# One decoder step on one core: the order of the projections before the attention, four accumulator banks for them, and a tanh written in place

## The chip, the cores and the metric

The kernel runs on one core of a Trainium2 chip. The metric is the device time of one execution in microseconds. Five engines work side by side, each through its own instructions in order: TensorE (PE: matrix products and transposes), VectorE (DVE), ScalarE (ACT), GpSimd (POOL) and SyncE (SP), which issues the DMA transfers.

## The reference

One layer of a decoder is computed for a new sequence of 1024 tokens and for 8 single tokens with caches. After an RMS norm, one projection gives all streams; a recurrence (RG-LRU) and a dilated attention run in parallel, each is gated, and both are merged:

```python
proj = xn @ w_in
u, z_rnn, q, k, v, z_attn, g_rnn, g_attn = jnp.split(proj, split_points(), axis=-1)
uc, conv_new = causal_conv(u, conv_buf, conv_w, conv_b)
h, h_last = rg_lru(uc, h0, lru_w_a, lru_b_a, lru_w_x, lru_b_x, lru_lambda)
y_rnn = (h * jax.nn.silu(z_rnn)) @ w_rnn_out
...
y_attn = (y_attn * jax.nn.silu(z_attn)) @ w_attn_out
mixed = jax.nn.sigmoid(g_rnn) * y_rnn + jax.nn.sigmoid(g_attn) * y_attn
out = rms_norm(mixed @ w_out, norm_post)
```

Everything is float32. u, z_rnn and the two gates have 1024 columns each, z_attn 512, and q, k, v 1536 each.

## The kernel before

**Stripes.** The 1032 tokens lie along the free axis. A projection is worked off in *stripes* of 128 columns of `w_in`. A stripe is 8 contraction steps times three chunks of tokens (256, 384 and 392 wide; four chunks of about 256 for the first stripes), and each step is three matmuls (`mm3`, line 146), since both operands are split into a rounded part and a rest (`whi`, `wlo`; `xh`, `xl`): 72 matmuls a stripe, 24 a chunk, 12 a half chunk. ScalarE and VectorE make `whi` and `wlo` out of the loaded weights (`wraw`, lines 225 and 226) one or two stripes ahead.

**Accumulators.** A chunk is summed in one of the eight PSUM banks. `ps_tile` hands them out by tag: 2 banks `pj` for the projections, 3 `s` and 2 `pt` and 1 `o` for the recurrence and the attention. A chunk's bank is free again when the chunk has been read: by one ScalarE copy for u (line 540), by a ScalarE sigmoid for a gate (line 1109), by a ScalarE sigmoid and a VectorE product for z and z_attn (lines 549/550 and 686/687).

**The chains.** The recurrence is four *chains* of two 128-channel blocks (`chain`, `chain_front`). A chain convolves u, computes two gates from it (12 pairs of matmuls into `ps_s`, each read by two ScalarE sigmoids, line 601), multiplies on POOL (line 606), takes tanh, exp and square roots on ScalarE (lines 608, 623, 627), some products on VectorE and POOL, and a scan on VectorE (line 641). ScalarE loads another function table (ACT_TABLE_LOAD) when it changes between sigmoid, exp and square root.

**What sets the order.** The program is recorded in one pass; each engine then runs its part in the recorded order. The stripes are the main line. Beside it lie *lanes* (generators: a chain, an attention head pair, a merge, the decoder's sample rows), and every `yield n` in a lane says that its next step is due n planner nanoseconds later. The planner's clock `clk` advances with every recorded matmul, by a cost formula in `mm`; `tick`, called once per half chunk, records every lane step that is due.

**Slots.** All working tiles lie in 42 equal slots (`Arena`). When none is free, `Arena.get` calls `force`, which records the next lane step at once, due or not, until a slot comes free:

```python
    def get(self, shape, dtype, name):
        while not self.slots:
            self.pump()
```

**The stages.** In the opening, four stripes of u run while the four token groups are normalised and transposed. Then come z 0 to 3, u 4 and 5, z 4 and 5, u 6 and 7, z 6 and 7, the four z_attn stripes, 6 gate stripes, 36 stripes of v, k, q with the attention of the head pairs in the lanes, 10 gate stripes, and the three output projections. Gates are spilled to memory and loaded again later.

## Time and profile before

| | |
|---|---|
| median of 3 runs | 1291.03 us (1291.01 to 1292.82) |
| the profiled execution: its own time | 1294.25 us |
| the profiled execution: span, first to last instruction | 1292.5 us |
| mean granted TensorE clock | 0.987 |
| busy: PE, DVE, ACT, POOL | 1258.5, 604.6, 553.2, 221.9 us |
| DMA over the span | mean 97 GB/s |

PE is busy for 97% of the span, so nearly all of the time is matmul work, and the rest of the time is found by asking where PE stands still or runs at a lower clock. Busy shares of the other engines are averages over stages that differ much from each other.

### The profile page before, as it was taken

What the parts mean: (1) busy time and instruction counts of PE and PEld (TensorE: products, weight loads), DVE (VectorE), ACT (ScalarE), POOL (GpSimd) and SP (SyncE); (2) the same over time, 40 slices, a digit from 0 to 9 for tenths busy, and PEclk for the clock granted to TensorE, in tenths of its full rate; (3) what the DMA queues carried; (4) which work ended last, traced back from release to release, by engine and by line L of the source; (5) the groups of instructions that cost most, each with busy time, mean ns of one, the idle gap of its engine ahead of it and who ended that gap; (6) DMA issues with size and microseconds to landing.
All of it is one profiled execution on the core that took longest, in us unless ns stands there. A gap on an engine that the chain in (4) does not pass through costs nothing.

```text
span 1292.5 us, 21498 instructions
## 1 busy us (share of the span) xinstructions
PE 1258.5 (97%) x8726; PEld 1209.8 (94%) x8726; DVE 604.6 (47%) x1323; ACT 553.2 (43%) x1231; POOL 221.9 (17%) x232
## 2 busy tenths in 40 slices
PE   8999999799999999999999999999999999999997
PEld 8999998789999989999999999999999999998997
DVE  5552472761574274544256324643345245554226
ACT  6536636445539744334334344333652331222222
POOL 5000221311220131150026001420026000002001
PEclk9999999899999999999999999999999999998999
DMA  7210130232330133632074016512365474223115
GB/s 234 67 33 17 33 99 17 71 125 69 100 112 5 49 96 108 165 84 66 17 212 120 25 42 164 135 50 66 97 189 154 137 260 150 66 66 99 33 67 197
DMA packets 149449, 125.98 MB, mean 97 GB/s; under 512 B 8873, under 2 KB 135305, under 8 KB 149342
## 3 DMA queue, kind: packets, MB, share of 16 engines
q1 hardware_dynamic: 149350, 124.61, 32.0%
q8 instruction: 69, 1.13, 0.4%
q14 instruction: 30, 0.25, 0.1%
HBM read 98.44 MB, written 26.21 MB: 96 GB/s over the span
## 4 chain that ended last, share of the span: by engine, by line
PE 87%; ACT 5%; DVE 5%; issue 1%; DMA 1%; POOL 0%; SPq 0%; DVEq 0%; ACTq 0%
PE ps_pj L146 75%; PE ps_s L146 5%; PE ps_o L146 3%; PE ps_s L150 3%; PE ps_pt L150 2%; ACT gate L601 1%; DVE wlo L226 1%; DVE tanh L641 1%; ACT whi L225 1%; DMA wraw<-in_w_in 1%; DVE ck L1057 1%; ACT gate L623 1%; ACT sq L627 0%; ACT P L823 0%; ACT L627 0%
## 5 line engine op out<-in xcount | busy, mean ns | idle before, releaser
L146 PE MATMUL ps_pj<-xh,whi 128*128 128x256 f32 (+3 forms) x1760 | 574.7, 327 | 12.1 <-DVE za L687 11.0
L146 PE MATMUL ps_pj<-xl,whi 128*128 128x256 f32 (+3 forms) x1760 | 560.4, 318 | 0.0
L146 PE MATMUL ps_pj<-xh,wlo 128*128 128x256 f32 (+3 forms) x1760 | 560.1, 318 | 0.0
L146 PEld LDWEIGHTS ps_pj<-xh,whi 128*128 128x128 f32 x1760 | 334.0, 190 | 21.0 <-DVE za L687 12.4
L146 PEld LDWEIGHTS ps_pj<-xl,whi 128*128 128x128 f32 x1760 | 334.0, 190 | 0.2
L146 PEld LDWEIGHTS ps_pj<-xh,wlo 128*128 128x128 f32 x1760 | 333.6, 190 | 0.0
L226 DVE TENSOR_TENSOR wlo<-wraw,whi 128x512 fp32r<-128x512 f32 x176 | 149.6, 852 | 320.0 <-ACT whi L225 314.0
L225 ACT ACTIVATE whi<-wraw 128x512 fp32r<-128x512 f32 x176 | 109.6, 625 | 3.9 <-DMA wraw<-in_w_in 1.9
L823 ACT ACTIVATE P<-P,stat 128x128 f32<-128x128 f32 (+1 forms) x192 | 84.3, 440 | 53.0 <-DVE stat L819 52.9
L146 PE MATMUL ps_pj<-wlo,mh 128*128 128x256 f32 (+1 forms) x288 | 80.6, 286 | 0.1
L146 PE MATMUL ps_pj<-whi,mh 128*128 128x256 f32 x256 | 73.3, 286 | 2.7 <-ACT whi L225 2.7
L146 PE MATMUL ps_pj<-whi,ml 128*128 128x256 f32 x256 | 73.2, 286 | 0.0
L716 ACT ACTIVATE qt<-ps_pj,qsc 128x384 f32<-128x384 f32 (+1 forms) x36 | 27.6, 766 | 81.5 <-PE ps_pj L146 79.6
L146 PE MATMUL ps_pj<-hzh,wlo 128*128 128x256 f32 (+2 forms) x192 | 61.4, 320 | 0.0
L146 PE MATMUL ps_pj<-hzl,whi 128*128 128x256 f32 (+2 forms) x192 | 61.4, 320 | 0.0
L146 PE MATMUL ps_pj<-hzh,whi 128*128 128x256 f32 (+2 forms) x192 | 61.3, 319 | 0.0
L1109 ACT ACTIVATE sg<-ps_pj 128x256 f32<-128x256 f32 (+2 forms) x48 | 22.0, 458 | 91.7 <-PE ps_pj L146 90.4
L819 DVE CUSTOM_DVE_ANT_0 P<-ps_s,base 128x128 f32<-128x128 f32 (+1 forms) x192 | 56.0, 348 | 8.5 <-PE ps_s L146 8.0
L840 ACT ACTIVATE PT<-ps_pt 128x256 f32<-128x256 f32 (+1 forms) x48 | 21.0, 437 | 91.0 <-PE ps_pt L150 90.9
L601 ACT ACTIVATE gate<-ps_s,par 64x256 f32<-64x256 f32 (+2 forms) x96 | 52.1, 543 | 16.0 <-PE ps_s L146 14.4
L838 DVE COPY PT<-ps_pt 128x512 f32<-128x512 f32 (+1 forms) x48 | 28.7, 597 | 54.1 <-PE ps_pt L150 54.1
L146 PEld LDWEIGHTS ps_pj<-wlo,mh 128*128 128x128 f32 (+1 forms) x288 | 52.3, 181 | 0.5 <-DVE wlo L226 0.4
(247 smaller groups left out, 1690.1 us busy)
## 6 DMA issues: line engine op xcount, KB each, us to landing
wraw<-in_w_in SPq DMA_DIRECT2D x72, 512.0 KB
ck<-in_cache_kv_w SPq DMA_DIRECT2D x24, 512.0 KB
sgd<-sg SPq DMA_DIRECT2D x16, 516.0 KB
sgl<-sgd SPq DMA_DIRECT2D x16, 516.0 KB
xin<-in_x_prompt SPq DMA_DIRECT2D x16, 512.0 KB
qb<-sd SPq DMA_DIRECT2D x12, 512.0 KB
fb<-fd SPq DMA_DIRECT2D x24, 256.0 KB
hzd<-uc SPq DMA_DIRECT2D x8, 516.0 KB
```

Of the source, the lines that this page charges most:

```text
L146: nc.tensor.matmul(out, lhsT, rhs, start=start, stop=stop)
L150: nc.tensor.transpose(out, in_, idn)
L225: nc.scalar.activation(hi[:, a:b], raw[:, a:b], AF.Copy)
L226: nc.vector.tensor_tensor(lo[:, a:b], raw[:, a:b], f32(hi[:, a:b]), op=OP.subtract)
L601: nc.scalar.activation(G[gate][rows, cs], p[at:at + 64, :n], AF.Sigmoid, bias=par[rows, b, 5 + gate:6 + gate])
L623: nc.scalar.activation(R[b], R[b], AF.Exp, scale=spk[:, 1, b:b + 1])
L716: nc.scalar.activation(dst, src, AF.Copy, scale=C["qsc"][:, g, hp:hp + 1])
L819: nc.vector.tensor_tensor_reduce(out=pt[:, h, :128 * n], in0=ps[h][:, off:off + 128 * n], in1=base, scale=-SLOPES[g][2 * hp + h] * DIL[g], ...
L823: nc.scalar.activation(pt[:, h, :128 * n], pt[:, h, :128 * n], AF.Exp, scale=-1.0, bias=st[:, g, 0, h, b:b + 1], accum_out=st[:, g, 1, h, ...
L838: nc.vector.tensor_copy(t, src)
L840: nc.scalar.activation(t, src, AF.Copy)
L1109: nc.scalar.activation(z[:, c0:c0 + n], p[:, :n], AF.Sigmoid)
```

## The change

**Order.** The opening runs u 0, u 1 and two gate stripes. After it, the list `EARLY_BLOCKS` alternates pairs: z, u, gates, z, u, gates and so on, with the z_attn stripes among the last z and gate stripes. A chain is spawned after each second u stripe as before. Eight gate stripes (instead of six) come before the attention, eight (instead of ten) after it.

**Banks.** Outside the attention (`wide[0]` true) the projections' chunks take the banks in turn from two `pj` and the two `pt` banks; during the attention they have the two `pj` banks as before.

**tanh in place.** tanh is written into the tile `gi` of the input gate, which the POOL product reads just ahead of it; before, it went into a fresh slot and `gi` was freed.

**Planner.** `mm` now charges n/2.25 + 4 instead of n/2.4 planner nanoseconds for a matmul of n columns, and the gate steps of a chain are due 1000 instead of 1300 after one another.

```diff
--- before.py
+++ after.py
@@ -24,13 +24,18 @@
 WIN = (128, 512, 2048)
 COL_U, COL_Z, COL_Q, COL_K, COL_V = 0, 1024, 2048, 3584, 5120
 COL_ZA, COL_GR, COL_GA = 6656, 7168, 8192
-UZ = ((COL_U, (0, 1, 2, 3)), (COL_Z, (0, 1, 2, 3)), (COL_U, (4, 5)), (COL_Z, (4, 5)), (COL_U, (6, 7)), (COL_Z, (6, 7)))
 EPS = 1e-6
 BIG = 1e30
 NSLOT = 42
 WARM = 40
-EARLY_GATES = 6
 GATES = [(kind, b) for kind in range(2) for b in range(8)]
+LATE_GATES = 8
+
+FIRST = [("u", 0), ("u", 1), ("g", 0), ("g", 1)]
+EARLY_BLOCKS = [("z", 0), ("z", 1), ("u", 2), ("u", 3), ("g", 2), ("g", 3),
+                ("z", 2), ("z", 3), ("u", 4), ("u", 5), ("g", 4), ("g", 5),
+                ("z", 4), ("z", 5), ("u", 6), ("u", 7), ("g", 6), ("a", 0),
+                ("z", 6), ("z", 7), ("a", 1), ("a", 2), ("a", 3), ("g", 7)]
 STEP = 3400
 SPARE = 5
 KY, VY = 3000, 4000
@@ -78,7 +83,13 @@
     ar = Arena(arena_pool, NSLOT)
     new = ar.get
 
+
+    wide, turns = [True], [0]
+
     def ps_tile(tag):
+        if tag == "pj" and wide[0]:
+            turns[0] += 1
+            tag = ("pj", "pj", "pt", "pt")[turns[0] % 4]
         bufs = {"pj": 2, "s": 3, "pt": 2, "o": 1}[tag]
         return psum.tile([128, 512], F32, tag=tag, bufs=bufs, name="ps_" + tag)
 
@@ -140,7 +151,7 @@
         for q in out.shape[1:]:
             n *= q
         if rhs.dtype == F32R:
-            clk[0] += n / 2.4 if n >= 256 else max(4 * n / 2.4, 107)
+            clk[0] += n / 2.25 + 4 if n >= 256 else max(4 * n / 2.4, 107)
         else:
             clk[0] += max(4 * n / 2.4, 214) * (0.75 if out.shape[0] == 64 else 1.0)
         nc.tensor.matmul(out, lhsT, rhs, start=start, stop=stop)
@@ -171,19 +182,19 @@
     w_ao = I["w_attn_out"][0].rearrange("(k p) c -> p k c", p=128)
     w_oo = I["w_out"][0].rearrange("(k p) c -> p k c", p=128)
     WL = []
-    for base, bl in UZ:
-        for b in bl:
-            WL.append(w_in[:, :, base + 128 * b:base + 128 * b + 128])
-    for hp in range(4):
-        WL.append(w_in[:, :, COL_ZA + 128 * hp:COL_ZA + 128 * hp + 128])
-    for kind, b in GATES[:EARLY_GATES]:
-        WL.append(w_in[:, :, (COL_GA, COL_GR)[kind] + 128 * b:][:, :, :128])
+    for what, i in FIRST + EARLY_BLOCKS:
+        if what == "g":
+            kind, b = GATES[i]
+            c = (COL_GA, COL_GR)[kind] + 128 * b
+        else:
+            c = {"u": COL_U, "z": COL_Z, "a": COL_ZA}[what] + 128 * i
+        WL.append(w_in[:, :, c:c + 128])
     for hp in range(4):
         for g in range(3):
             for base in (COL_V, COL_K, COL_Q):
                 c = base + g * 512 + hp * 128
                 WL.append(w_in[:, :, c:c + 128])
-    for kind, b in GATES[EARLY_GATES:]:
+    for kind, b in GATES[-LATE_GATES:]:
         WL.append(w_in[:, :, (COL_GA, COL_GR)[kind] + 128 * b:][:, :, :128])
     for s in range(4):
         WL.append(w_ao[:, :, 256 * s:256 * s + 256])
@@ -600,13 +611,12 @@
                     at = 64 * (gate ^ s)
                     nc.scalar.activation(G[gate][rows, cs], p[at:at + 64, :n], AF.Sigmoid,
                                          bias=par[rows, b, 5 + gate:6 + gate])
-                yield 1300
+                yield 1000
         ar.free(*xs)
         R[b], gi = G
         nc.gpsimd.tensor_tensor(x, x, gi, op=OP.mult)
-        t = T[b] = new([128, NT], F32, "tanh")
-        nc.scalar.activation(t, R[b], AF.Tanh, scale=spk[:, 0, b:b + 1])
-        ar.free(gi)
+        T[b] = gi
+        nc.scalar.activation(gi, R[b], AF.Tanh, scale=spk[:, 0, b:b + 1])
 
     def chain(j):
         bl = (2 * j, 2 * j + 1)
@@ -1102,12 +1112,12 @@
 
     sgd = dram.tile([2, KB, 128, NT], F32, name="sgd")
 
-    def proj_g(kind, b):
+    def proj_g(kind, b, chunks=CHUNKS):
         z = new([128, NT], F32, "sg")
 
         def evac(c0, n, p):
             nc.scalar.activation(z[:, c0:c0 + n], p[:, :n], AF.Sigmoid)
-        yield from project(evac)
+        yield from project(evac, chunks)
 
         def spill():
             nc.sync.dma_start(sgd[kind, b], z)
@@ -1137,7 +1147,7 @@
     def turned(gi, k0=0):
         ahead[:] = [lambda k: k >= k0 and next(norm[gi], None)]
 
-    started = [proj_u(b, EARLY) for b in range(4)]
+    started = [proj_u(0, EARLY), proj_u(1, EARLY), proj_g(*GATES[0], EARLY), proj_g(*GATES[1], EARLY)]
 
     def half(i, n=1):
         for _ in range(n):
@@ -1189,20 +1199,12 @@
     clear_low_w()
     C = late_consts()
     spawn("lru", chain(0))
-    for b in range(4):
-        advance(proj_z(b))
-    spawn("lru", chain(1))
-    for j in (2, 3):
-        for b in (2 * j, 2 * j + 1):
-            advance(proj_u(b))
-        for b in (2 * j, 2 * j + 1):
-            advance(proj_z(b))
-        spawn("lru", chain(j))
+    for what, i in EARLY_BLOCKS:
+        advance({"u": proj_u, "z": proj_z, "a": proj_za}[what](i) if what != "g" else proj_g(*GATES[i]))
+        if what == "u" and i % 2:
+            spawn("lru", chain(i // 2))
     spawn("lru", state_out())
-    for hp in range(4):
-        advance(proj_za(hp))
-    for kind, b in GATES[:EARLY_GATES]:
-        advance(proj_g(kind, b))
+    wide[0] = False
     for hp in range(4):
         for g in range(3):
             for kind in (2, 1, 0):
@@ -1218,11 +1220,12 @@
         nc.sync.dma_start(t, sgd[kind, b])
         sgt[kind, b] = t
 
-    for i, (kind, b) in enumerate(GATES[EARLY_GATES:]):
-        if i == len(GATES) - EARLY_GATES - 2:
+    for i, (kind, b) in enumerate(GATES[-LATE_GATES:]):
+        if i == LATE_GATES - 2:
             until(lambda: len(merged) == 4 and len(sampled) == 4)
             spawn("split", split_ya())
-        if i == len(GATES) - EARLY_GATES - 3:
+            wide[0] = True
+        if i == LATE_GATES - 3:
             load_sg(0, 0)
             load_sg(0, 1)
         advance(proj_g(kind, b))
```

**Order on TensorE, second chain.** `uc2` is the convolved u split in two, `lh` and `low_w` the recurrence's weights, `whi`, `wlo`, `xh` and `xl` the projection's operands; the number at the end of a name counts tiles. Before, among the last pairs of gate matmuls of the second chain:

```order
L146 MATMUL ps_pj_2301<-xh7_24_123,wlo_124_2125 128x392
L146 MATMUL ps_s_2333<-uc2_120_2090,lh_1976 128x392
L146 MATMUL ps_s_2333<-uc2_120_2090,low_w0_135 128x392
L146 MATMUL ps_s_2341<-uc2_125_2174,lh_2035 128x392
L146 MATMUL ps_s_2341<-uc2_125_2174,low_w1_136 128x392
L146 MATMUL ps_s_2346<-uc2_121_2091,lh_1976 128x256
L146 MATMUL ps_s_2346<-uc2_121_2091,low_w0_135 128x256
L146 MATMUL ps_s_2351<-uc2_126_2175,lh_2035 128x256
L146 MATMUL ps_s_2351<-uc2_126_2175,low_w1_136 128x256
L146 MATMUL ps_s_2356<-uc2_121_2091,lh_1976 128x384
L146 MATMUL ps_s_2356<-uc2_121_2091,low_w0_135 128x384
L146 MATMUL ps_s_2361<-uc2_126_2175,lh_2035 128x384
```

Now, the chain's first pair:

```order
L157 MATMUL ps_pt_2158<-xh3_20_119,whi_117_2028 128x384
L157 MATMUL ps_pt_2158<-xl3_28_127,whi_117_2028 128x384
L157 MATMUL ps_pt_2158<-xh3_20_119,wlo_118_2029 128x384
L157 MATMUL ps_s_2175<-uc2_114_2006,lh_1906 128x256
L157 MATMUL ps_s_2175<-uc2_114_2006,low_w0_135 128x256
L157 MATMUL ps_pt_2158<-xh4_21_120,whi_117_2028 128x384
L157 MATMUL ps_pt_2158<-xl4_29_128,whi_117_2028 128x384
L157 MATMUL ps_pt_2158<-xh4_21_120,wlo_118_2029 128x384
L157 MATMUL ps_pt_2158<-xh5_22_121,whi_117_2028 128x384
```

Before, eight pairs in a row stand at this place without a projection matmul between them (`Arena.get` found no slot free there, in the first z_attn stripe). Now each pair is followed by the 12 projection matmuls of a half chunk, through the whole of the second chain.

**Order on ScalarE, after the gates of a chain.** `zs` and `za` are the z and z_attn chunks read from the accumulator; `ps_pj` or `ps_pt` names the kind of bank. Before, second chain:

```order
L601 ACTIVATE gate_133_2276<-ps_s_2371,par_114 64x392
L608 ACTIVATE tanh_136_2377<-gate_130_2253,spk_132 128x1032
L608 ACTIVATE tanh_137_2380<-gate_132_2275,spk_132 128x1032
L225 ACTIVATE whi_138_2382<-wraw_135_2339 128x512
L686 ACTIVATE za_134_2338<-ps_pj_2384 128x256
L623 ACT_TABLE_LOAD
L623 ACTIVATE gate_130_2253<-gate_130_2253,spk_132 128x1032
L623 ACTIVATE gate_132_2275<-gate_132_2275,spk_132 128x1032
L225 ACTIVATE whi_138_2382<-wraw_135_2339 128x512
L686 ACT_TABLE_LOAD
L686 ACTIVATE za_134_2338<-ps_pj_2415 128x384
L627 ACT_TABLE_LOAD
```

Now, the same chain:

```order
L612 ACTIVATE gate_129_2194<-ps_s_2390,par_114 64x392
L236 ACTIVATE whi_134_2353<-wraw_125_2128 128x512
L619 ACTIVATE gate_127_2174<-gate_126_2173,spk_132 128x1032
L619 ACTIVATE gate_129_2194<-gate_128_2193,spk_132 128x1032
L560 ACTIVATE zs_133_2352<-ps_pj_2395 128x384
L633 ACT_TABLE_LOAD
L633 ACTIVATE gate_126_2173<-gate_126_2173,spk_132 128x1032
L633 ACTIVATE gate_128_2193<-gate_128_2193,spk_132 128x1032
L560 ACT_TABLE_LOAD
L560 ACTIVATE zs_133_2352<-ps_pj_2428 128x392
L236 ACTIVATE whi_138_2460<-wraw_137_2458 128x512
L637 ACT_TABLE_LOAD
```

The functions and the reads of chunks come in the same pattern, with the tanh's output now named as a gate tile, and the chunks now come out of both kinds of bank.

**Order on ScalarE, opening.** `ext` is a chunk of u, `sg` a chunk of a gate, `xin` normalised rows, `xh0` to `xh2` the transposed ones that PE works with. Before:

```order
L243 ACTIVATE whi_47_334<-wraw_10_94 128x512 x2
L370 ACTIVATE xin_7_88<-xin_7_88,rstd_326 128x512 x2
L540 ACTIVATE ext_40_244<-ps_pj_313 128x256
L540 ACTIVATE ext_41_246<-ps_pj_359 128x256
L379 ACTIVATE xh0_17_116<-ps_s_388,gain_115 128x256
L379 ACTIVATE xh1_18_117<-ps_s_396,gain_115 128x256
```

Now:

```order
L254 ACTIVATE whi_45_330<-wraw_10_94 128x512 x2
L381 ACTIVATE xin_7_88<-xin_7_88,rstd_322 128x512 x2
L551 ACTIVATE ext_40_244<-ps_pt_309 128x256
L1119 ACT_TABLE_LOAD
L1119 ACTIVATE sg_47_353<-ps_pj_356 128x256
L390 ACTIVATE xh0_17_116<-ps_s_386,gain_115 128x256
L390 ACTIVATE xh1_18_117<-ps_s_394,gain_115 128x256
```

The read of the third stripe's chunk is a sigmoid now, with a table load ahead of it, and both stand ahead of the `xh` tiles. In the opening there are five such loads now after the first two of the program, and one before (line 504).

## Rows read from the trace of the kernel before

**Rows 1.** The page, part 1: busy time and share of the span.
```profile
PE 1258.5 (97%) x8726; PEld 1209.8 (94%) x8726; DVE 604.6 (47%) x1323; ACT 553.2 (43%) x1231; POOL 221.9 (17%) x232
```

**Rows 2.** What TensorE waited for: in total, times, longest.
```profile
PE ps_pj L146 <- DVE za L687: 11.0, 5, 4.9
PE ps_s L146 <- ACT gate L601: 2.7, 5, 0.7
PE ps_pj L146 <- ACT whi L225: 2.7, 1, 2.7
PE ps_pt L150 <- ACT P L823: 2.3, 2, 2.2
...
PE ps_pj L146 <- ACT ext L540: 0.6, 1, 0.6
```

**Rows 3.** Windows (us): length; busy (instructions) of PE, PEld, DVE, ACT, POOL; clock; DMA.
```profile
150.00:175.00 25.00, 25.00 (x159) 25.00 (x158) 19.95 (x24) 6.36 (x14) 11.05 (x6) 1.00 0.27 81
200.00:225.00 25.00, 22.32 (x131) 20.95 (x130) 3.50 (x6) 17.94 (x33) 3.38 (x2) 0.93 0.07 22
225.00:250.00 25.00, 18.16 (x102) 17.64 (x101) 15.93 (x14) 13.44 (x17) 8.52 (x4) 0.88 0.12 43
250.00:275.00 25.00, 21.05 (x123) 20.53 (x122) 20.18 (x26) 7.74 (x13) 8.74 (x12) 0.92 0.52 169
450.00:475.00 25.00, 22.57 (x158) 19.66 (x158) 19.36 (x45) 12.79 (x36) 6.70 (x4) 0.93 0.18 52
```

**Rows 4.** Timeline of ScalarE, second chain: start, us, instruction, [idle before <- releaser].
```profile
213.62 9.13 ACT L601 ACTIVATE gate<-ps_s,par 64x392 f32<-64x392 f32 x16
...
224.89 0.62 ACT L225 ACTIVATE whi<-wraw 128x512 fp32r<-128x512 f32 x1
...
225.79 1.28 ACT L623 ACT_TABLE_LOAD   x1
...
227.08 2.21 ACT L623 ACTIVATE gate<-gate,spk 128x1032 f32<-128x1032 f32 x2
```

**Rows 5.** Timelines of ScalarE and VectorE: one z_attn chunk behind a scan.
```profile
241.92 0.49 ACT L686 ACTIVATE za<-ps_pj 128x384 f32<-128x384 f32 x1 [3.85 <-PE ps_pj L146]
...
246.68 4.13 DVE L641 TENSOR_TENSOR_SCAN tanh<-gate,sq 128x1024 f32<-128x1024 f32 x1
...
251.59 0.55 DVE L687 TENSOR_TENSOR za<-ps_pj,za 128x384 f32<-128x384 f32 x1
```

**Rows 6.** Timelines of POOL and ScalarE: product and tanh, first chain.
```profile
134.22 2.42 POOL L606 TENSOR_TENSOR uc<-uc,gate 128x1032 f32<-128x1032 f32 x1 [0.31 <-ACT gate L601]
...
135.85 2.19 ACT L608 ACTIVATE tanh<-gate,spk 128x1032 f32<-128x1032 f32 x2
```

**Rows 7.** Timelines of ScalarE and TensorE, opening.
```profile
25.55 1.63 ACT L379 ACTIVATE xh<-ps_s,gain 128x256 fp32r<-128x256 f32 x3 [0.29 <-PE ps_s L150]
...
24.67 0.38 PE L146 MATMUL ps_pj<-xh,whi 128*128 128x256 f32 x1 [0.56 <-ACT ext L540]
```

**Rows 8.** Timelines of TensorE and ScalarE: one pair of attention blocks.
```profile
545.92 1.13 PE L146 MATMUL ps_s<-kt,qt 64*128 64x256 f32 x8
...
549.11 0.49 ACT L823 ACTIVATE P<-P,stat 128x256 f32<-128x256 f32 x1
...
551.77 1.04 PE L150 MATMUL ps_pt<-ident,P 128*128 128x128 f32 x8
```

**Rows 9.** Timeline of ScalarE, fourth chain within the attention.
```profile
448.77 2.02 ACT L627 ACTIVATE sq<-tanh 128x1032 f32<-128x1032 f32 x2
```

**Rows 10.** Timelines of POOL and VectorE: the decoder's value products.
```profile
826.86 5.74 POOL L1054 TENSOR_TENSOR ck<-ck,pT 128x1024 f32<-128x1024 f32 x3 [17.93 <-DVE yn L1047]
...
842.90 3.40 DVE L1057 TENSOR_TENSOR ck<-ck,ck 128x1024 f32<-128x1024 f32 x1
```

**Rows 11.** Chain of waits, in order of time: half chunks of 12 matmuls.
```profile
391.33 1.42 PE ps_pj L146 x12
...
392.99 2.11 PE ps_pj L146 x12
```

## The prediction

> **What bounds the kernel.** I read four views in turn. The page's first part: TensorE (PE) is busy for 97% of the span, the other engines for 47% at most [rows 1]. So a change that leaves the matmuls alone can only win what PE loses in waits and at a lower clock. PE's waits name the losses: 11.0 us in five waits for VectorE's product of a z_attn chunk, 2.7 us for the gates' sigmoids, 2.7 us for a `whi`, 2.3 us for the attention's exponentials, 0.6 us for a copy of u [rows 2]. The windows say where: between 200 and 275 us PE's busy time falls to 22.32, 18.16 and 21.05 of 25 us and the granted clock to 0.93, 0.88 and 0.92; before that, at 150 to 175 us, PE is busy throughout at clock 1.00 although VectorE is busy for 19.95 us [rows 3]. There is a second, smaller hole at 450 to 475 us. The timelines say why. Sixteen gate sigmoids stand in one block of 9.13 us on ScalarE [rows 4], because the order recorded the chain's last pairs of gate matmuls back to back. The chain's products and scans then follow as densely on VectorE: the sigmoid of a z_attn chunk ends at 242.4 us, but its product starts only at 251.59, behind a scan of 4.13 us that began at 246.68 [rows 5]. With two banks for the projections, PE cannot start the next chunk but one before that product is done.
>
> **The change, part by part.** The sum is made against the profiled execution's 1294.25 us; the median of the runs shown, 1291.03, lies 3.2 us lower, and I take the difference over to it.
>
> *The hole at 200 to 275 us.* At full pace a window holds 159 matmuls, 0.157 us each; these three hold 131, 102 and 123, so 477 - 356 = 121 are missing: 19.0 us [rows 3]. Of it 13.5 us is PE's idle time, the rest the clock. The new order has one pair of gate matmuls per half chunk through the whole second chain, so the block of sixteen sigmoids is gone, and with it the dense run of products behind it. The slots that it lacked come from the tanh in place (one a block, two a chain), and from gate stripes, whose tile leaves soon, between z stripes, whose tile stays until its chain ends. Bounds: nothing, if the same work blocks elsewhere; 19.0 if all comes back. I take 19.0 off, and put back what is left in the next item.
>
> *What is left of it.* ScalarE and VectorE have the same work for the chains. The longest stretch of ScalarE without a chunk's read is now `whi`, load, two square roots and load: 0.62 + 1.28 + 2.02 + 1.28 = 5.2 us [rows 4, 9]. Two banks let PE run ahead by one chunk, two half chunks of 1.42 to 2.11 us [rows 11]; four banks by three chunks, over 8.5 us. So PE does not wait for reads; it may wait for a `wlo` behind two scans of 4.13 us. I take 1.0 us; bounds 0 and 5.
>
> *The opening.* Two gate stripes there change their reads from copies to sigmoids, between groups whose norm needs a square root: four more table loads of 1.28 us [rows 4]. ScalarE is the pace there: it waits 0.29 us between `xh` tiles, and PE lives on them [rows 7]. The first load stands directly ahead of the `xh` of the second group and I count it whole; the others fall where ScalarE waits anyway. PE's wait of 0.56 us for a bank [rows 7] goes, with four of them. With half a microsecond for the other loads: +1.3 us; bounds -0.6 and 4 x 1.28 = 5.1. The Trainium skill ("ScalarE: Activation LUTs", What ACT_TABLE_LOAD costs) speaks against this edit: it says to group functions by table set, and puts a switch at about 2.66 us, load and drain. By that figure the four loads would come to 10.6 us, and the sum to 3.6 us saved. The trace does not agree on the second half: the load at 225.79 ends at 227.07 and the exponential starts at 227.08 [rows 4].
>
> *tanh in place.* ScalarE must now wait until POOL has read `gi`. In the first chain the second product runs from 134.22 to 136.64, so the first is done before that; the two tanh, 2.19 us together, start at 135.85 and so at about 136.9 [rows 6]: each after its product. Cost 0; bound, where the tanh come right behind the last gate: 0.31 + 2.42 less the first tanh's 1.1 and a `whi`'s 0.6, 1.0 us a chain. The cover is the four banks; in the fourth chain, with two, it is counted below.
>
> *The fourth chain and the first attention heads.* Before, PE loses 2.43 us of busy time and 7% of the clock in 25 us, 1.75 us, here: 4.2 us [rows 3]. The chain still runs into the attention. Now its tanh, exponentials and square roots stand between the exponentials of the first head pair's own blocks. Following ScalarE from the first scores in the new order: two gate sigmoids 1.1 (9.13 / 16 each), load 1.3, four exponentials 2.0 [rows 8], load 1.3, sigmoids 1.1, `whi` 0.6, two tanh 2.2 with an estimated wait of 1.0 for POOL (the bound above), a copy as long as an exponential 0.5, load 1.3, four exponentials 2.0 [rows 4, 6]: the second pair of blocks is ready after 14.4 us, and PE wants it after two turns of 4.7 us [rows 8], at 9.4. That is an estimated 5.0 us of waits less half a microsecond that the scores take, and the same 1.75 us of clock: about 6.3, so +2.1 us; with a little for the blocks behind the square roots I take +2.3. Bounds: -4.2 (fewer loads in all, and the hole closes) and +8.
>
> *The attention's pace.* The planner charged 256 / 2.4 = 107 ns for a matmul that takes 1.42 us / 12 = 118 [rows 11]; now it charges 118. So every lane step comes about a tenth sooner. A pair of blocks has 4.7 us between its scores' end (547.05) and its turn (551.77), and is ready at 549.6: 2.2 us of slack [rows 8], of which half a microsecond goes. Cost 0, bounds 0 and 4. In one head pair the order runs out of slots and takes three of the decoder's sample steps early; VectorE's sum of 3.40 us then waits for POOL's products, 5.74 us for three [rows 10]. It holds a chunk's copy and one pair's scores: +1.5 us, bounds 0 and 4.
>
> *After the attention.* Two gate stripes fewer (72 x 0.157 = 11.3 us each) cover the last merge; no wait of PE for it is among the rows of its waits, the largest of which are in [rows 2]. If that cover is gone, up to 3 us. Cost 0. The four banks there save nothing, since PE has no wait for a chunk's read left.
>
> **Sum:** -19.0 + 1.0 + 1.3 + 2.3 + 1.5 = -12.9 us: 1281.4 for a profiled execution, **1278** for the median of the runs.
>
> **The rivals.**
> - *More comes back* (0.15): the fourth chain's hole closes too, since the program has 6 table loads fewer around it. 1291.0 - 19.0 + 1.0 + 1.3 + 1.5 - 4.2 = 1272. For it: the loads, 1.28 us each [rows 4]. Against: ScalarE has the chain's and the attention's functions at once, with two banks.
> - *The jam moves* (0.12): ScalarE's and VectorE's work is the same, and half of the loss turns up at another chain: 9.5 less is saved, 1287.6. For it: VectorE at 20 of 25 us [rows 3]. Against: the first chain has such a window with no loss, and only two banks.
> - *The order is not relieved* (0.03): slots run out again later in the early stripes, the block returns, and the opening's and the attention's costs remain: about 1294. The order speaks against it.
> - *Slower, by the attention's pace* (0.04): if blocks become ready later than 2.2 us more than now, PE waits in each of the 48 turns. From 12.9 / 48 = 0.27 us a turn on, the gain is eaten; at 0.35 us it is 1295. For it: the lanes come sooner while a block's work stays. Against: slack of four times what is taken.
> - *Loads cost double* (0.03): ScalarE stands for as long again behind each of the opening's four loads, 8 x 1.28 = 10.2 us instead of 1.3: 1287. The two rows at 225.79 and 227.08 [rows 4] speak against it. This is the time by the Trainium skill's page named above.
>
> **How the numbers follow.** My forecast has 0.63, around 1278, from 1273 to 1284. The range 1269 to 1288 takes in the bounds of the unknown costs as far as they are likely together, and most of the first two rivals; the rest leave out some 0.17. A measurement of this kernel can tell about 0.2%, 2.6 us, from no change. Below 1288.4 lie the forecast, the first rival, two thirds of the second, and part of the last: 0.88. Within 0.2%: a third of the second, parts of the third and of the last: 0.07. Slower: the fourth and the rest: 0.05.
>
> **What would show it.** Right: the windows between 75 and 330 us all hold PE at 24.5 us or more at clock 1.00, the wait for the z_attn product is gone from PE's waits, no block of sixteen sigmoids is left; the opening's first four stripes end one to two microseconds later; PE's waits for exponentials near the first heads grow to some 5 us. Wrong: a window below 23 us in the early stripes (the jam moved), or many short waits of PE for exponentials through the attention (its pace).

## The result, and the profile after

The changed kernel takes **1279.71 us** (median of 4 runs, 1275.84 to 1280.51), the kernel before 1291.11 in the same comparison: a ratio of 0.9903, 95% interval 0.988 to 0.9925. It is faster by about 11 us. The profiled execution took 1279.06 us with a span of 1277.3. Against the span of before, 1292.5 us, that is 15.2 us less; the profiled execution of before lay 3.2 us above its median, which is why the spans differ by more than the medians.

The page, part 1, and what TensorE (PE) waited for, after; they answer to [rows 1] and [rows 2]:

```profile
PE 1251.2 (98%) x8726; PEld 1205.4 (94%) x8726; DVE 613.2 (48%) x1323; ACT 549.9 (43%) x1230; POOL 219.0 (17%) x232
```

```profile
PE ps_s L157 <- DVE ck L1067: 4.4, 1, 4.4
PE ps_s L161 <- DVE xl L391: 2.8, 2, 1.7
...
PE ps_s L161 <- DVE vn L769: 1.6, 1, 1.6
...
PE ps_pt L161 <- ACT P L833: 0.4, 1, 0.4
```

The 11.0 us for the z_attn product are gone, and so are the gates' 2.7 but for 0.8 and the exponentials' 2.3 but for 0.4. At the top stands a wait that is new: 4.4 us for `ck`, VectorE's sum of the decoder's value products (line 1067). Windows of after (columns as in [rows 3]):

```profile
200.00:225.00 25.00, 25.00 (x160) 25.00 (x159) 3.74 (x6) 17.59 (x31) 5.25 (x2) 1.00 0.31 97
225.00:250.00 25.00, 25.00 (x162) 25.00 (x161) 15.65 (x16) 14.41 (x21) 5.19 (x3) 1.00 0.10 30
250.00:275.00 25.00, 25.00 (x165) 25.00 (x164) 22.42 (x24) 10.07 (x18) 8.84 (x11) 1.00 0.41 127
...
450.00:475.00 25.00, 25.00 (x196) 22.51 (x195) 11.21 (x36) 10.38 (x33) 0.00 (x0) 1.00 0.33 91
...
975.00:1000.00 25.00, 20.62 (x107) 20.27 (x106) 14.48 (x11) 2.79 (x6) 10.86 (x4) 0.80 0.32 105
```

Both holes of [rows 3] are closed: the three windows from 200 us and the one at 450 us are full, at a granted clock of 1.00. A new hole is at 975 us, with a clock of 0.80. The same window of before had lost much less:

```profile
975.00:1000.00 25.00, 24.58 (x153) 24.19 (x152) 13.98 (x10) 3.92 (x8) 16.18 (x6) 0.93 0.41 129
```

**Where the time came from** is read from landmarks, instructions that both programs have. After has two gate stripes more ahead of the attention and two fewer behind it. One stripe takes 11.31 us, read from the same chunk of two gate stripes that follow each other, after:

```profile
967.31 0.49 ACT L1119 ACTIVATE sg<-ps_pj 128x384 f32<-128x384 f32 x1 [3.31 <-PE ps_pj L157]
...
978.62 0.49 ACT L1119 ACTIVATE sg<-ps_pj 128x384 f32<-128x384 f32 x1 [3.24 <-PE ps_pj L157]
```

So 22.6 us are allowed for the two. The landmarks are the last group's first `xh` (end of the opening), the first read of a query stripe, the read of the single tokens' queries in the 3rd, 10th, 11th and 12th query stripes, and the first product with `w_attn_out`. ScalarE's timeline and the tile `yah`, before:

```profile
49.04 0.48 ACT L379 ACTIVATE xh<-ps_s,gain 128x264 fp32r<-128x264 f32 x1
...
379.98 0.47 ACT L716 ACTIVATE qt<-ps_pj,qsc 128x256 f32<-128x256 f32 x1 [1.62 <-PE ps_pj L146]
...
491.68 0.22 ACT L718 ACTIVATE smp<-ps_pj 128x8 f32<-128x8 f32 x1
...
817.56 0.17 ACT L718 ACTIVATE smp<-ps_pj 128x8 f32<-128x8 f32 x1
...
868.35 0.22 ACT L718 ACTIVATE smp<-ps_pj 128x8 f32<-128x8 f32 x1
...
914.01 0.21 ACT L718 ACTIVATE smp<-ps_pj 128x8 f32<-128x8 f32 x1
...
L146 PE MATMUL ps_pj<-yah,whi x96: 274/337/345, 1042.5 to 1087.4; 128*128 128x256 f32 x32, 128*128 128x384 f32 x32, 128*128 128x392 f32 x32
```

And after:

```profile
49.12 0.48 ACT L390 ACTIVATE xh<-ps_s,gain 128x264 fp32r<-128x264 f32 x1
...
382.01 0.47 ACT L726 ACTIVATE qt<-ps_pj,qsc 128x256 f32<-128x256 f32 x1 [0.22 <-PE ps_pj L157]
...
489.88 0.21 ACT L728 ACTIVATE smp<-ps_pj 128x8 f32<-128x8 f32 x1
...
816.92 0.17 ACT L728 ACTIVATE smp<-ps_pj 128x8 f32<-128x8 f32 x1
...
869.07 0.22 ACT L728 ACTIVATE smp<-ps_pj 128x8 f32<-128x8 f32 x1
...
914.67 0.21 ACT L728 ACTIVATE smp<-ps_pj 128x8 f32<-128x8 f32 x1
...
L157 PE MATMUL ps_pj<-yah,whi x48: 278/337/343, 1027.7 to 1072.5; 128*128 128x256 f32 x16, 128*128 128x384 f32 x16, 128*128 128x392 f32 x16
```

| stretch | before, us | after, us | difference | predicted |
|---|---|---|---|---|
| to the end of the opening | 49.0 | 49.1 | +0.1 | +1.3 |
| to the first query read | 330.9 | 332.9 less 22.6 | -20.7 | -18.0 |
| to the 3rd query stripe (first heads, fourth chain) | 111.7 | 107.9 | -3.8 | +2.3 |
| to the 10th (attention) | 325.9 | 327.0 | +1.2 | 0 |
| to the 11th (sample event) | 50.8 | 52.2 | +1.4 | +1.5 |
| to the 12th | 45.7 | 45.6 | -0.1 | 0 |
| to `w_attn_out` (end of the attention) | 128.5 less 22.6 | 113.0 | **+7.1** | 0 |
| to the end of the span | 250.0 | 249.6 | -0.4 | 0 |
| sum | | | -15.2 | -12.9 |

Two of these stretches don't hold the same matmuls before and after. The rows from the first query read to the 3rd query stripe, before and after (columns as in [rows 3]), have 768 and 757 matmuls:

```profile
379.98:491.68 111.70, 109.26 (x768) 101.30 (x766) 51.64 (x117) 75.57 (x151) 15.17 (x8) 0.98 0.15 46
```

```profile
382.01:489.88 107.87, 106.43 (x757) 98.31 (x756) 51.30 (x113) 59.74 (x133) 17.78 (x8) 1.00 0.19 57
```

The stretch ahead holds 10 more, once the 144 of the two gate stripes are taken off: the lanes' matmuls come sooner. At the prediction's 0.157 us a matmul that is 1.7 and 1.6 us of work which only moved. Without it the early stripes won some 22.3 us, and the first heads some 2.1.

So the early stripes gave 4 us more than was predicted, the first heads gained where a loss of 2.3 us was predicted, and the end of the attention lost 7.1 us that the sum did not hold. Timelines of VectorE and PE at that place, after, show the loss:

```profile
974.73 2.96 DVE L237 TENSOR_TENSOR wlo<-wraw,whi 128x512 fp32r<-128x512 f32 x1 [9.95 <-DMA sgd<-sg]
...
983.74 3.36 DVE L1067 TENSOR_TENSOR ck<-ck,ck 128x1024 f32<-128x1024 f32 x1
...
987.24 3.54 PE L157 MATMUL ps_s<-one,ck 128*128 128x1 f32 x16 [4.38 <-DVE ck L1067]
```

Sixteen matmuls of one column (eight in the code, sixteen records in the trace) need VectorE's second sum, which ends at 987.1. PE reaches them at 982.86 and stands for 4.38 us; then the clock is low, 0.66, 0.50 and 0.82 in the windows of 5 us from 985 us on:

```profile
985.00:990.00 5.00, 2.76 (x13) 2.79 (x14) 2.10 (x1) 0.00 (x0) 1.01 (x1) 0.66 0.67 176
990.00:995.00 5.00, 5.00 (x24) 5.00 (x25) 1.28 (x5) 0.00 (x0) 0.00 (x0) 0.50 0.38 141
995.00:1000.00 5.00, 5.00 (x28) 4.96 (x27) 1.11 (x2) 0.90 (x2) 0.00 (x0) 0.82 0.00 0
```

VectorE itself stood still: it waited 9.95 us for the slot of a weight's low half, whose earlier tenant, a gate, was still on its way to memory. Before, PE came to the same sixteen when the sum was nearly done; there, too, the clock was lower behind them, 0.66 in the window from 990 us:

```profile
989.28 1.92 PE L146 MATMUL ps_s<-one,ck 128*128 128x1 f32 x16 [0.42 <-DVE ck L1057]
```

```profile
990.00:995.00 5.00, 5.00 (x26) 4.90 (x25) 2.46 (x5) 0.00 (x0) 1.34 (x1) 0.66 0.36 105
```

Counted from the read in the 12th query stripe, the second sum ends after 75.1 us before and after 72.4 us now; PE comes to it after 74.9 us before and after 68.2 us now. So it is not the sum that comes later than before, but PE that comes sooner.

### The profile page after: what moved, and what is told of

Read it like the earlier page. It is cut to its first block, busy times and chain, and to the rows that moved or that the text cites. A ratio compares the mean times of both kernels' runs of the same rounds, so it can differ in the third digit from the quotient of the medians.

```text
span 1277.3 us, 21495 instructions
## 1 busy us (share of the span) xinstructions
PE 1251.2 (98%) x8726; PEld 1205.4 (94%) x8726; DVE 613.2 (48%) x1323; ACT 549.9 (43%) x1230; POOL 219.0 (17%) x232
## 5 line engine op out<-in xcount | busy, mean ns | idle before, releaser
L157 PE MATMUL ps_pj<-xh,whi 128*128 128x256 f32 (+2 forms) x1384 | 453.0, 327 | 0.0
L157 PE MATMUL ps_pj<-xl,whi 128*128 128x256 f32 (+2 forms) x1384 | 441.3, 319 | 0.0
L157 PE MATMUL ps_pj<-xh,wlo 128*128 128x256 f32 (+2 forms) x1384 | 441.0, 319 | 0.2 <-DVE wlo L250 0.2
L157 PEld LDWEIGHTS ps_pj<-xh,whi 128*128 128x128 f32 x1384 | 261.8, 189 | 6.2 <-issue 5.5
L157 PEld LDWEIGHTS ps_pj<-xh,wlo 128*128 128x128 f32 x1384 | 261.4, 189 | 0.5 <-DVE wlo L250 0.5
L157 PEld LDWEIGHTS ps_pj<-xl,whi 128*128 128x128 f32 x1384 | 261.7, 189 | 0.1
L157 PE MATMUL ps_pt<-xh,whi 128*128 128x256 f32 (+3 forms) x376 | 117.9, 314 | 0.0
L157 PE MATMUL ps_pt<-xl,whi 128*128 128x256 f32 (+3 forms) x376 | 117.3, 312 | 0.0
L157 PE MATMUL ps_pt<-xh,wlo 128*128 128x256 f32 (+3 forms) x376 | 117.3, 312 | 0.0
L157 PEld LDWEIGHTS ps_pt<-xl,whi 128*128 128x128 f32 x376 | 70.7, 188 | 0.1
```

Source lines behind the costliest of these rows:

```text
L157: nc.tensor.matmul(out, lhsT, rhs, start=start, stop=stop)
```

## The experiments

The theory at the outset: the new order saves the time, since slots no longer run out; banks and tanh add little; the new wait is the price of the planner's costs, by which lane steps are recorded sooner against the matmuls. The rivals: the four banks save it; the two gate stripes that the end lacks make the wait; the table loads of the opening cost more than they seem to.

**1. The order alone.** The changed kernel with the other three parts undone:

```diff
-    wide, turns = [True], [0]
+    wide, turns = [False], [0]
...
-        T[b] = gi
-        nc.scalar.activation(gi, R[b], AF.Tanh, scale=spk[:, 0, b:b + 1])
+        t = T[b] = new([128, NT], F32, "tanh")
+        nc.scalar.activation(t, R[b], AF.Tanh, scale=spk[:, 0, b:b + 1])
+        ar.free(gi)
...
-            clk[0] += n / 2.25 + 4 if n >= 256 else max(4 * n / 2.4, 107)
+            clk[0] += n / 2.4 if n >= 256 else max(4 * n / 2.4, 107)
...
-                yield 1000
+                yield 1300
...
-            wide[0] = True
```

> The kernel before with the new order alone: u, z, gate and z_attn stripes alternate and eight gate stripes come late, but two banks for the projections, the tanh in a tile of its own, and the old planner costs. Theory 1 (the order): the slots no longer run out in the second chain, so the block of sixteen gate sigmoids is gone and nearly all of the early gain, some 20 us in the two traces, is there with the order alone; the end of the attention loses as little as in the kernel before, since the steps come as late as there: 1271 to 1280 us. Rival (the banks): the order spreads the chains, but with two banks PE still waits for reads behind scans and square roots; half of the gain is missing: 1282 to 1288 us, with waits of PE for reads of the projections in the early windows.

Measured: 1283.3 us, ratio 0.9922 (0.9907 to 0.9937). That is the rival's range. PE's waits:

```profile
PE ps_pj L157 <- ACT sg L1120: 2.1, 1, 2.1
PE ps_pt L161 <- ACT P L834: 2.1, 1, 2.1
PE ps_pj L157 <- DVE za L698: 2.0, 1, 2.0
PE ps_pj L157 <- DVE zs L561: 1.0, 3, 0.6
```

The order removes the long block, and with it the hole: the three windows from 200 us have 25.00 us of PE each, with 161, 160 and 158 matmuls at a clock of 1.00. But with two banks PE waits for reads of z and z_attn chunks elsewhere in the early stripes (2.0 us at 353 us) and of a gate's chunk behind the attention (2.1 us at 1015 us), and it loses at the first heads: the window at 450 us has 22.87 us of PE at a clock of 0.86.

**2. Everything but the order.** Before, with four banks, tanh in place and the new costs (the same edits, the other way).

> The kernel before with everything but the order: four banks outside the attention, tanh in place, the new planner costs, on the old order of stripes with six early gates. Theory 1 (the order): the slots still run out in the first z_attn stripe (the recording then takes ten steps of the chain early instead of fourteen), the block of gate sigmoids stays, PE loses 10 to 19 us between 200 and 275 us again, and the time is 1284 to 1292 us. Rival (the banks): with three chunks of read-ahead the block of 9.13 us is covered, the hole shrinks to under 5 us and the time is 1275 to 1281 us.

Measured: 1289.91 us, ratio 0.9987 (0.9975 to 1.0). The time falls where theory 1 put it. Its reason holds in part (a block of 18 sigmoids, 10.28 us, is still there), but most of the loss is elsewhere:

```profile
PE ps_s L151 <- DVE ck L1061: 4.4, 1, 4.4
```

```profile
200.00:225.00 25.00, 22.05 (x128) 20.15 (x127) 2.85 (x5) 22.06 (x32) 4.80 (x2) 0.93 0.07 22
225.00:250.00 25.00, 23.07 (x145) 22.66 (x144) 22.67 (x24) 7.08 (x14) 11.17 (x7) 1.00 0.26 83
250.00:275.00 25.00, 25.00 (x160) 25.00 (x159) 21.41 (x28) 13.74 (x22) 3.76 (x10) 1.00 0.47 152
```

The three windows lack 477 - 433 = 44 matmuls, 7 us, where before lacked 121. So the banks, the tanh and the costs together cover more than half of the hole on the old order as well, and neither theory's figure for it (10 to 19 us, under 5) came out. The gain is eaten at the end: the wait for `ck` is there in full, 4.4 us. This kernel has ten gate stripes after the attention, not eight. So the wait does not come from the two stripes that the end lacks.

**3. The decoder's last products recorded later.** The changed kernel with one line changed in `sample`, ahead of the sixteen matmuls:

```diff
-        yield 3000
+        yield 9000 if hp == 3 else 3000
         p = ps_tile("s")
         for b in range(DB):
             mm(p[:, b:b + 1], acc[:, b], C["one1"], start=True, stop=True)
```

> The changed kernel, but the last decoder head pair's 16 small matmuls that read the sum of the value products are recorded 6 us later (a delay of 9000 in place of 3000 for that pair alone). Theory 1: they stand too early on PE; PE reaches them 4.4 us before VectorE's sum is done, and the clock falls behind the wait; recorded later they find the sum done, the wait is gone and with it some 7 us: 1271 to 1275 us, clock 1.00 between 980 and 1000 us. Rival: the loss is VectorE's, which is behind for want of slots (a weight's low half waits for a gate's store); PE then meets the next late thing and the loss moves on: 1278 to 1281 us.

Measured: **1268.83 us** (1266.99 to 1270.93), ratio 0.9813 (0.9797 to 0.9829), 11 us under the changed kernel and below the expected range. One window, and the timelines of VectorE and PE:

```profile
975.00:1000.00 25.00, 25.00 (x165) 24.78 (x164) 16.60 (x17) 6.73 (x12) 10.08 (x4) 1.00 0.36 118
```

```profile
974.83 1.98 DVE L237 TENSOR_TENSOR wlo<-wraw,whi 128x512 fp32r<-128x512 f32 x1 [11.27 <-DMA sgd<-sg]
...
982.91 3.40 DVE L1067 TENSOR_TENSOR ck<-ck,ck 128x1024 f32<-128x1024 f32 x1
...
986.46 1.92 PE L157 MATMUL ps_s<-one,ck 128*128 128x1 f32 x16
```

VectorE is as late as in the changed kernel: it waits 11.27 us for the slot, and its second sum ends at 986.3. PE has other work until then, and the window is full at a clock of 1.00. The rival falls: VectorE's lateness matters only because PE was sent to the sum too early. The stretch from the 12th query stripe to `w_attn_out` (1017.6 - 913.44) takes 104.2 us against 113.0; that is 8.8 of the 10.9 us by which the spans differ, and 1.2 lie ahead of the 12th. Before it took 128.5 less 22.6, 105.9 us, so the later sum also takes away 1.7 us that before lost there.

**4. The opening as before.** FIRST is u 0 to u 3, and g 0, g 1 stand where u 2, u 3 stood. First on the changed kernel:

> The changed kernel with the opening as before: u stripes 0 to 3 start it, and the two gate stripes that started it stand where u stripes 2 and 3 stood. Theory 1: the four table loads of the opening cost 1.0 us by the traces (the first of them stands ahead of the xh of the second group, the rest are covered): 1278 to 1280 us, the same within what can be told. Rival (loads cost double and all are uncovered): 5 to 10 us come back: 1270 to 1275 us. Second rival (the swap disturbs the first chain, whose partner stripes come later): 1281 to 1285 us.

Measured: 1277.05 us (1273.01 to 1280.81), ratio 0.9877 (0.9857 to 0.9896), between the two. But its wait for `ck` was 2.1 us, not 4.4, which could make all of the difference. So once more with experiment 3's later sum in both:

> The changed kernel with the later sum, and with the opening as before (u stripes 0 to 3 start it, the two gate stripes follow where u stripes 2 and 3 stood). Theory 1: the better median of the run with the old opening came from a shorter wait at the end of the attention, which the later sum takes away; the four table loads of the opening cost about 1.0 us: 1266 to 1270 us, within what can be told of the 1268.8 us of the later sum alone. Rival (the opening's gates cost 2.5 us or more, as the medians of the two runs read at their face value): 1263 to 1266 us.

Measured: 1269.63 us (1265.89 to 1271.77), ratio 0.9823 (0.9799 to 0.9847): the same as experiment 3's 0.9813. The gates in the opening cost nothing that can be told, and the better median above fits the shorter wait at the end.

**5. The old costs.** The changed kernel with the planner's lines of experiment 1 alone (n / 2.4 and `yield 1300`).

> The changed kernel with the planner's old costs (256 / 2.4 ns for a matmul, 1300 between the half chunks of a chain); order, four banks and tanh in place as changed. Theory 1 (the costs): the end's wait of 4.4 us comes from the truer cost, by which every step of a lane is recorded a tenth sooner against the matmuls; with the old cost it shrinks to about what the kernel before had there, and 5 us come back; but the fourth chain runs later into the attention, and most of what the change gained there (5 us between the second and the third head's queries) is lost again. Together within 3 us of the changed kernel: 1277 to 1283 us, no wait of PE for the sum of the value products over 1 us, the window at 450 us under 24 us of PE. Rival (the two gate stripes that the end lacks made the wait): the wait of 4 us stays, 1283 to 1287 us. Second rival (the banks and tanh closed the fourth chain's hole, not the costs): 1272 to 1275 us.

Measured: 1276.3 us (1271.26 to 1278.0), ratio 0.9867 (0.9842 to 0.9893); slightly under the expected range. No wait for `ck` is left. PE waits for exponentials instead, and the hole at 450 us is back:

```profile
PE ps_pt L161 <- ACT P L833: 4.3, 3, 2.2
```

```profile
450.00:475.00 25.00, 22.55 (x165) 19.66 (x164) 18.96 (x44) 14.83 (x38) 5.86 (x4) 1.00 0.15 44
```

Two of the three waits, 2.3 us, stand at the first heads (at 459 us) and are as long as before's; the third, 2.0 us at 852 us, falls into the stretch of the sample event, which takes 54.6 us against 52.2, and I did not follow its cause. From the first to the third query stripe's read of the single tokens it takes 492.55 - 389.50 = 103.1 us; the changed kernel 489.88 - 392.17 = 97.7; before 491.68 - 388.97 = 102.7. These stretches hold 715, 698 and 716 matmuls, so about half of each difference is work that moved: 2.7 us of loss come back with the old costs, where before lost 2.2 more than the changed kernel. The old costs also put the fourth chain back where it was: its tanh starts at 438.46 us, in the changed kernel at 401.59. So on the new order the costs closed the fourth chain's hole; the banks and the tanh are not needed for it (97.7 us again in experiment 7, 98.3 in 9). The costs alone do not do it: on the old order, in experiment 2, the stretch takes 101.6 us with 701 matmuls.

The costs also opened the hole at the end: 104.6 us (920.00 to 1024.6) without them, 113.0 with. The other runs agree: with the new costs and the old delay PE waits for `ck` 4.4 us (the changed kernel, experiment 2) or 2.1 (experiment 4, the first run); with the old costs 0.4 (before) or not at all by the trace (experiments 1, 5 and 8).

**6. The distance between half chunks alone** (`yield 1300` on experiment 3's kernel):

> The changed kernel with the later sum, and with the old distance of 1300 between the half chunks of a chain; the new cost of a matmul stays. Theory 1: what closed the fourth chain's hole at the first heads is the cost of a matmul, by which all lanes come a tenth sooner; the distance alone matters little: 1267 to 1271 us. Rival (the distance of 1000 ends each chain earlier, and without it the fourth chain runs into the heads again): 1272 to 1275 us, the waits of PE for the heads' exponentials back at 4 us.

Measured: 1269.5 us, ratio 0.9826 (0.9807 to 0.9846), the same as experiment 3. The stretch at the first heads takes 488.92 - 391.17 = 97.8 us, as with 1000. At the end of the attention, too, nothing differs: the second sum ends at 986.4 us and the sixteen matmuls start at 986.55, with 1000 at 986.3 and 986.46. What is left of the two costs is the price of a matmul.

**7. Two banks** (experiment 3's kernel, `wide` false throughout):

> The changed kernel with the later sum, and with two banks for the projections everywhere. Theory 1 (the banks give the last third): with the order alone PE kept waits of 0.6 to 2.0 us for reads of the z and z_attn chunks, and its traces stood 5.5 us behind the changed kernel's at the first queries; without the banks the time is 1272 to 1277 us, with waits of PE for zs, za and sg among its largest. Rival (the new costs spread the chain's steps so that two banks do): 1267 to 1271 us, no such wait over 1 us.

Measured: 1279.48 us, ratio 0.9899 (0.9881 to 0.9917), 10.7 us above experiment 3 and more than I expected. Between the profiled executions it is 10.3 us: 6.7 in the stretch from the opening to the first query read (339.6 us against 332.9, with the same matmuls), 2.1 in the opening, which has two banks here as well, and 1.0 behind the attention. PE's waits for reads are there:

```profile
PE ps_pj L157 <- DVE zs L561: 2.3, 3, 1.2
PE ps_pj L157 <- DVE za L697: 2.0, 3, 1.1
```

**8. Four banks alone on the kernel before:**

> The kernel before with one edit: the projections cycle four banks outside the attention; old order, old costs, tanh in a tile of its own. Theory 1: the banks cover half of the hole by themselves (with everything but the order the hole was 10 us smaller): PE's 11 us of waits for the product of a z_attn chunk fall to under 3 us, and since the old costs leave the end as it was, the time is 1279 to 1284 us. Rival (it was the costs or the tanh that made the hole smaller there): 1287 to 1292 us, the wait for the z_attn product stays near 11 us.

Measured: 1281.2 us (1279.58 to 1283.17), ratio 0.9912 (0.9894 to 0.9931): in the median this one edit gives as much as the whole change. The block of sixteen sigmoids stays, and the wait for the z_attn product is gone; PE now waits for weights' low halves, which stand behind the chain's products (2.7 us) and behind a scan (3.6 us) on VectorE:

```profile
PE ps_pj L151 <- DVE wlo L231: 6.3, 2, 3.6
```

The three windows from 200 us hold 130, 118 and 147 matmuls, so 82 are still missing where before lacked 121.

**9. tanh in a tile of its own** (experiment 3's kernel):

> The changed kernel with the later sum, and with the tanh in a tile of its own again. Theory 1: the planner's order is the same with and without it (no slot runs out either way in the chains), and each tanh finds POOL's product done: no difference, 1267 to 1271 us. Rival (the wait for POOL costs ScalarE up to a microsecond a chain, and that reaches PE where two banks cover): 1264 to 1267 us. Second rival (the slot held longer makes weights' halves wait): 1272 to 1276 us.

Measured: 1270.13 us (1269.48 to 1271.63), ratio 0.9828 (0.9811 to 0.9844): no difference from experiment 3 that can be told.

The ratios side by side: banks alone 0.9912, order alone 0.9922, order with banks and tanh 0.9867, the whole change 0.9903, the whole change with the later sum 0.9813. Each of the two main parts gives about 10 us by itself. Together (with the tanh) they give some 17, and the truer price of a matmul takes some 4 back (the two intervals overlap a little) as long as the decoder's last products are not moved with it. In the early stripes alone the parts are not equal. From the opening to the first query read the whole change saves 22.3 us; the order with two banks some 16 (339.6 us, 6.1 more than the changed kernel after 4 matmuls more are taken off); the banks on the old order 8.6 (322.3 us against 330.9, with the same matmuls).

## Why the prediction was right, and where errors cancelled

The time was predicted at 1278.0 us and measured at 1279.71, inside the range. By steps:

- *The hole at 200 to 275 us, and what is left of it* (-19.0 and +1.0): right in place and in mechanism, too small in size: measured -20.7 together between the landmarks, -22.3 with the moved matmuls. That is above the bound of 19.0: the three windows of after hold 487 matmuls, ten more than the 477 that the sum took for full, and part of the gain lies outside them. The order alone closes the hole (experiment 1), as the prediction said; that slots were the reason for the block rests on the recorded order, since no run gave the old order more slots. What the prediction did not price apart is the cover of the four banks: without it PE loses 6 to 7 us more in the early stripes (experiments 1 and 7), and on the old order the banks alone save 8.6 us there, where PE then waits for `wlo`. The whole gain takes both. The Trainium skill ("Perfetto Trace Analysis", Matmul Optimizations) says to use all eight PSUM banks, so that more work can overlap; experiment 8 agrees with that rule, at a ratio of 0.9912 for two banks that stood unused outside the attention.
- *The opening* (+1.3): measured +0.1 between the spans, and experiment 4 shows no cost that can be told. The wait that was counted is there: behind the first load PE waits 1.1 us for `xl` of the second group, at 26.25 us, which no run with the old opening does. But the landmark scatters by more than that: with four banks it lies at 48.1 to 50.3 us in five profiled executions with the gates, and at 48.1 to 49.9 in four with u. (After's other 1.7 us for `xl` stand at 12.6 us, ahead of all these loads.) The doubled price of a table load, a rival at 0.03, is out: undoing the opening's gates on experiment 3's kernel should then have won some 10 us, and won none; and in after's trace the load at 23.63 us lasts 1.28 us, and the sigmoid behind it starts at 24.93. The Trainium skill ("ScalarE: Activation LUTs", What ACT_TABLE_LOAD costs) states that price, 2.66 us a switch with its drain; these runs do not agree with it here.
- *tanh in place* (0): right, by 9. Nor did the slots need it.
- *The fourth chain and the first heads* (+2.3): wrong, measured -3.8, of which 1.7 are moved matmuls, so some -2.1. The sign that PE's waits for exponentials grow to some 5 us did not show: 0.41 us. The walk along ScalarE was good: the second pair's exponentials are done 14.5 us after the first scores, predicted 14.4. The step that failed is the other side, "PE wants it after two turns of 4.7 us [rows 8], at 9.4": PE comes to the pair after 12.8 us. The row's 4.7 us run from the end of the scores, so two turns leave out the scores themselves and the first pair's transposes, 2.8 us here. And PE starts when the first of the four exponentials is done, not the last. PE and ScalarE, after:

```profile
393.71 0.93 PE L157 MATMUL ps_s<-kt,qt 64*128 64x128 f32 x8
...
406.93 1.92 PE L161 MATMUL ps_pt<-ident,P 128*128 128x128 f32 x8 [0.41 <-ACT P L833]
...
406.27 0.51 ACT L833 ACTIVATE P<-P,stat 128x256 f32<-128x256 f32 x1
...
414.20 2.02 ACT L637 ACTIVATE sq<-gate 128x1032 f32<-128x1032 f32 x2
```

With that wait the sum also kept the old loss of clock; but the chain's square roots now start at 414.20 us, where [rows 9] had them at 448.77, so the hole at 450 us has no chain left in it. Between the 1st and the 3rd query stripe ScalarE loads a table 5 times, before 11 times, and with the old costs (experiment 5) 11 times again. This is the term's lower bound, "fewer loads in all, and the hole closes".
- *The attention's pace* (0, bounds 0 and 4): measured +1.2, inside. *The sample event* (+1.5): measured +1.4, and the wait of 1.6 us for `vn` is the row that shows it.
- *After the attention* (0, up to 3 "if that cover is gone"): wrong, measured +7.1, outside its bounds. The term looked at the merge and at the cover of the late gate stripes. It was neither: experiment 2 has the two stripes and the same wait of 4.4 us. The missing piece was the price of a matmul, which the term did not apply to this place. The delays in `sample`, 4000 after each product and 3000 before the last matmuls, stayed as they were under the old price. At the new price a delay covers a tenth fewer matmuls, and PE arrived before VectorE's second sum. (Experiment 5 undid price and distance together, but by experiment 6 the distance moves nothing at this place.) In the rows of before a wait of 0.42 us at this very place told that nothing was to spare there; it was too small to stand among [rows 2], and I did not look for it. The clock then cost nearly as much as the wait.

That the time came out so near is partly luck: with the moved matmuls put back, the early stripes and the first heads each gave some 4 us more than the sum held, and the end of the attention took 7.1 us that it did not. Of the rivals, *more comes back* (1272, at 0.15) was right on its mechanism, the fourth chain's hole closed, and on its reason, six table loads fewer; only the end kept the time from it, and experiment 3, without that loss, is at 1268.83. *The jam moves* (1287.6, at 0.12) was right that a loss would turn up elsewhere, but not where or why: it is no other chain's. What I do not know is why VectorE's wait for the gate's store is so long (9.95 us, with SyncE behind other transfers); no run tried it, since moving PE made it harmless. And the median of before moved by 1.4 us between comparisons (1291.11 to 1292.55), so differences of 1 us between experiments settle nothing.

## What to carry to other kernels

When a planner's cost is made truer, every delay that was set by hand against the old cost changes its meaning; go through all of them, and first through those where the trace shows even a few tenths of a microsecond of waiting, since there the slack is used up. When stretches of two programs are compared between landmarks, count the matmuls between them: here 11 that had moved were nearly half of a difference of 3.8 us. When a read-ahead is short of buffers, try the unused accumulator banks first: here that one edit equalled, in the median, a reordering of the whole front of the program, though in the early stripes the order gave about twice as much. And a stall of the bounding engine is priced with the clock behind it, not by its length alone.

## What the runs showed of the hardware

- The sixteen matmuls of one column took 3.54 us after the wait of 4.38 us and 1.92 us without it (both rows above). The granted clock fell to 0.50 in the window from 990 us, the lower of its two levels (1.2 and 2.4 GHz) throughout, though PE was busy again from 987.24. Before, behind a wait of 0.42 us, it was 0.66 in the window from 990 us; in experiment 3, with no wait, the whole window from 975 to 1000 us is at 1.00. Wait and clock together made the stretch 8.8 us longer than in experiment 3.
- A subtraction for half a weight stripe on VectorE (128x512, `wlo`) took 2.96 us at 974.73 beside POOL's products on `ot` (970.03 to 977.14), and 0.69 us at 961.19 with POOL idle (the row below, after). Not every product of POOL does it: beside those on `ck` (962.29 to 968.47) one at 964.03 took 0.74 us.

```profile
961.19 0.69 DVE L237 TENSOR_TENSOR wlo<-wraw,whi 128x512 fp32r<-128x512 f32 x1 [1.31 <-ACT whi L236]
```
